# A batched matmul minus a tensor: the first eight tiles' transfers one by one in turn, transposes of tiles 3 and 4 moved into the head, and matmuls on zeros ahead of the first work

## The chip, the cores and the metric

The kernel runs on one core of one Trainium2 chip. The metric is the device time of one execution in microseconds (us); three runs of the kernel before gave a median of 220.35 us (220.28 to 220.97). A core has a matrix engine (TensorE, "PE" in the profile, its weight loads listed apart as "PEld"), a vector engine (VectorE, "DVE"), a scalar engine (ScalarE, "ACT"), GpSimd ("POOL") and a queue processor (SyncE, "SP") that here issues every transfer. 16 DMA engines move data between the chip's main memory and on-chip memory. Each engine works through its own list in order and waits on semaphores for the others.

## The reference

```python
batch, m, k, n = 16, 512, 1024, 768
# x: (16, 512, 1024), weight: (1024, 768), sub_value: (16, 512, 768), all float32
def reference(x, weight, sub_value):
    return (np.matmul(x, weight) - sub_value).astype(np.float32)
```

The 16 x 512 rows are one list of 8192 rows. The kernel casts x and the weight to 16-bit floats, multiplies with 32-bit sums and subtracts in 32 bits.

## The kernel before

**Tiles.** The 8192 rows are 64 "m tiles" of 128 rows, numbered mi from 0 to 63. Four of them are a group g, the unit of most transfers: a group of x is 2048 KB, of sub and of the output 1536 KB each, a single tile of x 512 KB and of sub 384 KB. The weight comes in four pieces (c from 0 to 3) of 768 KB; `load_w` (line 72) loads one and lets VectorE cast its two halves (line 76). The contraction of 1024 is done in four chunks c, each against one weight piece.

**One m tile** passes through five steps. `cast` (line 94): ScalarE turns the tile of x into 16-bit floats. `transposes` (line 100): TensorE transposes it in four pieces, each a multiplication with an identity matrix (line 105), into a PSUM buffer (`psum_t`, two of them); behind the fourth, ScalarE copies the result to on-chip memory (`xt_tile`, line 112). `matmuls(mi, c)` (line 128): four matmuls of 384 columns for one chunk, 16 for a tile, summed into one of three `psum_o` buffers (line 133). `finish` (line 141): VectorE subtracts, reading `psum_o` and the tile of sub and writing the result over the tile of sub (`so_tile`, line 144). `store` (line 90) sends a group of these out.

**The order** on each engine is the order in which the program names the steps; nothing is rearranged between `keep` calls. First SyncE's list of transfers is named (lines 149 to 162): x tile 0, then the weight pieces with x tiles 1 and 2 between them, x tile 3, sub 0 and 1, x 4 and 5, and so on in pairs and then in groups. Then the head (lines 164 to 183): tiles 0 to 2 (HEAD is 3) are cast, transposed and multiplied chunk by chunk as weight pieces come; when all 48 matmuls of the three are named, their subtractions follow, then cast and transposes of tiles 3 and 4, then the casts of 5 and 6. Then the tile loop (line 186), from tile 3 on: the four chunks of tile mi with one transpose piece of tile mi + 2 behind each, the copy of that tile, the cast of tile mi + 4, and the subtraction of tile mi.

**Transfers in the loop.** At the start of group g the loop names the load of x group g + 3, of sub group g + 2 and the store of group g - 1 (XA, SA, OA are 3, 2, 1). A load waits until its buffer is free (four for groups of x, six shared by sub groups and weight pieces), a store for the subtraction of the group's last tile. Besides, each transfer waits for the landing of the one eight places before it in SyncE's list, since eight semaphores are used in turn.

**The end.** The last group is stored as two tiles, one tile and one tile.

Of the kernel before, what the change touches and what calls it, by code (L numbers as in the profile page):

```python
# [8 lines left out]
P = 128  # L9
Q = 32  # L10
F32 = mybir.dt.float32
F16 = mybir.dt.float16

S = 8
G = 4
XA, SA, OA = 3, 2, 1
TA = 2
CA = 2
HEAD = 3
ON_DVE = frozenset()  # L20


@with_exitstack
def kernel(
    ctx: ExitStack,
    tc: tile.TileContext,
    x: bass.AP,
    weight: bass.AP,
    sub_value: bass.AP,
    out: bass.AP,  # L30
):
    nc = tc.nc
# [12 lines left out]
    n_c = KW // P  # L45

    x_s = x_flat.rearrange("(s p j) k -> s p j k", p=P, j=S)
    sub_s = sub_flat.rearrange("(s p j) n -> s p j n", p=P, j=S)
    out_s = out_flat.rearrange("(s p j) n -> s p j n", p=P, j=S)
    w_c = weight.rearrange("(c p r) n -> c p r n", p=P, r=2)  # L50

    def rows(view, mi, n):
        return view[mi // S][:, mi % S : mi % S + n]

    const_pool = ctx.enter_context(tc.tile_pool(name="const", bufs=1))
    w_pool = ctx.enter_context(tc.tile_pool(name="w_pool", bufs=1))
    x_pool = ctx.enter_context(tc.tile_pool(name="x_pool", bufs=4))
    x16_pool = ctx.enter_context(tc.tile_pool(name="x16_pool", bufs=CA + 2))
    xt_pool = ctx.enter_context(tc.tile_pool(name="xt_pool", bufs=TA + 3))
    so_pool = ctx.enter_context(tc.tile_pool(name="so_pool", bufs=6))  # L60
    psum_t_pool = ctx.enter_context(tc.tile_pool(name="psum_t", bufs=2, space=bass.MemoryType.PSUM))
    psum_o_pool = ctx.enter_context(tc.tile_pool(name="psum_o", bufs=3, space=bass.MemoryType.PSUM))

    ident = const_pool.tile([P, P], F32)
    make_identity(nc, ident)


    w_sb = w_pool.tile([P, n_c, 2, N], F16)

    x_t, so_t, x16_t, xt_t, ps_t, po_t = {}, {}, {}, {}, {}, {}  # L70

    def load_w(c):
        st = so_pool.tile([P, 2, N], F32, name="w_stage", tag="so_tile")
        keep(nc.sync.dma_start(out=st, in_=w_c[c]))
        for r in range(2):
            keep(nc.vector.tensor_copy(out=w_sb[:, c, r], in_=st[:, r]))  # L76

    def load_x(mi, n):
        g, j = divmod(mi, G)
        if j == 0:  # L80
            x_t[g] = x_pool.tile([P, G, K], F32, name="x_tile")
        keep(nc.sync.dma_start(out=x_t[g][:, j : j + n], in_=rows(x_s, mi, n)))

    def load_sub(mi, n):
        g, j = divmod(mi, G)
        if j == 0:
            so_t[g] = so_pool.tile([P, G, N], F32, name="so_tile")
        keep(nc.sync.dma_start(out=so_t[g][:, j : j + n], in_=rows(sub_s, mi, n)))

    def store(mi, n):  # L90
        g, j = divmod(mi, G)
        keep(nc.sync.dma_start(out=rows(out_s, mi, n), in_=so_t[g][:, j : j + n]))

    def cast(mi):
        g, j = divmod(mi, G)
        x16_t[mi] = x16_pool.tile([P, K], F16, name="x16_tile")
        keep(nc.scalar.copy(out=x16_t[mi], in_=x_t[g][:, j]))  # L97


    def transposes(mi):  # L100
        def one(c):
            def f():
                if c == 0:
                    ps_t[mi] = psum_t_pool.tile([P, K], F16, name="psum_t")
                keep(nc.tensor.transpose(  # L105
                    ps_t[mi].bitcast(F32)[:, c * P : (c + 1) * P],
                    x16_t[mi].bitcast(F32)[:, c * P : (c + 1) * P],
                    ident,
                ))
                if c == n_c - 1:  # L110
                    xt_t[mi] = xt_pool.tile([P, K], F16, name="xt_tile")
                    keep(nc.scalar.copy(out=xt_t[mi], in_=ps_t.pop(mi)))  # L112
                    x16_t.pop(mi)
            return f
        return [one(c) for c in range(n_c)]

    def transposes_dve(mi):
        xt_t[mi] = xt_pool.tile([P, K], F16, name="xt_tile")
        src = x16_t.pop(mi).bitcast(F32).rearrange("p (c q) -> p c q", c=n_c)
        dst = xt_t[mi].bitcast(F32).rearrange("p (c m) -> p c m", c=n_c)  # L120
        for a in range(P // Q):
            for b in range(P // Q):
                keep(nc.vector.transpose(
                    dst[b * Q : (b + 1) * Q, :, a * Q : (a + 1) * Q],
                    src[a * Q : (a + 1) * Q, :, b * Q : (b + 1) * Q],
                ))

    def matmuls(mi, c):
        if c == 0:
            po_t[mi] = psum_o_pool.tile([P, 2, 512], F32, name="psum_o")  # L130
        for r in range(2):
            for h in range(2):
                keep(nc.tensor.matmul(  # L133
                    po_t[mi][:, h, :NS],
                    xt_t[mi][:, 2 * P * c + r : 2 * P * (c + 1) : 2],
                    w_sb[:, c, r, h * NS : (h + 1) * NS],
                    start=(c == 0 and r == 0),
                    stop=(c == n_c - 1 and r == 1),
                ))

    def finish(mi):
        g, j = divmod(mi, G)
        o = so_t[g][:, j].rearrange("p (h n) -> p h n", h=2)
        keep(nc.vector.tensor_tensor(  # L144
            out=o, in0=po_t.pop(mi)[:, :, :NS], in1=o, op=mybir.AluOpType.subtract
        ))


    load_x(0, 1)
    for c in range(n_c):  # L150
        load_w(c)
        if c < 2:
            load_x(c + 1, 1)
    load_x(3, 1)
    load_sub(0, 2)
    load_x(4, 2)
    load_sub(2, 2)
    load_x(6, 2)
    for g in range(2, XA):
        load_x(g * G, G)  # L160
        if g - 1 < SA:
            load_sub((g - 1) * G, G)

    for mi in range(HEAD):
        cast(mi)
        for f in transposes(mi):
            f()
        for c in range(max(mi, 1)):
            matmuls(mi, c)
        if mi:  # L170
            for t in range(mi + 1):
                matmuls(t, mi)
    for c in range(HEAD, n_c):
        for mi in range(HEAD):
            matmuls(mi, c)
    for mi in range(HEAD):
        finish(mi)
    for mi in range(HEAD, HEAD + TA):
        cast(mi)
        for f in transposes(mi):  # L180
            f()
    for mi in range(HEAD + TA, HEAD + TA + CA):
        cast(mi)


    for mi in range(HEAD, n_mt):
        g, j = divmod(mi, G)
        if j == 0 or mi == HEAD:
            if g + XA < n_g:
                load_x((g + XA) * G, G)  # L190
            if g + SA < n_g:
                load_sub((g + SA) * G, G)
            if g >= OA:
                store((g - OA) * G, G)
        t = mi + TA
        tr = []
        if t < n_mt and t not in ON_DVE:
            tr = transposes(t)
        for c in range(n_c):
            matmuls(mi, c)  # L200
            if tr:
                tr[c]()
        if mi + TA + CA < n_mt:
            cast(mi + TA + CA)
        finish(mi)
        if t + 1 < n_mt and t + 1 in ON_DVE:
            transposes_dve(t + 1)
    for g in range(n_g - OA, n_g - 1):
        store(g * G, G)
    store(n_mt - G, G - 2)  # L210
    store(n_mt - 2, 1)
    store(n_mt - 1, 1)
# [30 lines left out]
```

## Time and profile before

| | |
|---|---|
| median of three runs | 220.35 us (220.28 to 220.97) |
| profiled execution: its time, its span | 221.13 us, 219.4 us |
| mean granted TensorE clock | 0.982 |
| busy: PE, ACT, DVE | 202.2 us (92%), 126.7 us (58%), 65.2 us (30%) |
| read from main memory, written | 61.87 MB, 25.17 MB |
| a chunk matmul (line 133), mean | 332 ns, x1024 |
| a transpose piece (line 105), mean | 282 ns, x256 |
| a cast (line 97), a copy (line 112), a subtraction (line 144), mean | 1048 ns, 1012 ns, 958 ns, x64 each |

The span is the time from the first to the last instruction that the profiler recorded; the execution's own time is a little longer. Matmuls are pipelined, so the time shown for one is longer than the distance from one to the next, and a group's length (first start to last end) divided by its count is the better price. The page cuts the span into 40 slices of 5.5 us with a digit for each engine's busy tenths; the granted clock of TensorE has its own row there.

### The profile page before, as it was taken

To read this page: it belongs to the slowest core of one execution; us is meant where nothing else is said; L and a number is where in the kernel's file an instruction comes from. 1 tells how busy PE (TensorE), PEld (TensorE's weight loads), DVE (VectorE), ACT (ScalarE), POOL (GpSimd) and SP (SyncE) were. 2 spreads that over 40 slices of the span, in tenths; PEclk is the share of its full clock that TensorE was granted. 3 is DMA by queue.
4 is the path that set the end of the run, shared out by engine and by line. 5 is a ranking of instruction groups with operands and counts; after the bars stand their busy time and mean duration, and the time that the engine had idled before them with its cause. 6 is when DMAs were issued, how large, how long until landed. Compare 5 with 4: busy or idle time off the path is not lost.

```text
span 219.4 us, 3000 instructions
## 1 busy us (share of the span) xinstructions
PE 202.2 (92%) x1280; PEld 138.3 (63%) x1280; DVE 65.2 (30%) x72; ACT 126.7 (58%) x129; POOL 0.7 (0%) x6
## 2 busy tenths in 40 slices
PE   0687589999999999999999999999999999999991
PEld 0344356677667766677667766677667766676660
DVE  0330403322333323333233332233322333223331
ACT  3523526666766667666667666676666766667510
POOL 1000000000000000000000000000000000000000
PEclk9999958999999999999999999999999999999999
DMA  6999999999999999999999999999999999995543
GB/s 226 422 416 420 438 427 416 432 426 418 423 419 429 423 430 427 426 425 435 427 428 430 426 417 428 435 426 424 425 434 407 429 433 426 424 424 211 251 179 143
DMA packets 8509, 87.22 MB, mean 398 GB/s; under 512 B 944, under 2 KB 944, under 8 KB 2608
## 3 DMA queue, kind: packets, MB, share of 16 engines
q1 hardware_dynamic: 8496, 87.04, 94.4%
q8 instruction: 10, 0.16, 0.3%
q14 instruction: 3, 0.02, 0.0%
HBM read 61.87 MB, written 25.17 MB: 397 GB/s over the span
## 4 chain that ended last, share of the span: by engine, by line
PE 92%; ACT 3%; DMA 2%; issue 1%; DVE 0%
PE psum_o L133 78%; PE psum_t L105 14%; DMA x_tile<-in_x_dram 2%; ACT x_tile L97 1%; ACT xt_tile L112 1%; DVE so_tile L144 0%
## 5 line engine op out<-in xcount | busy, mean ns | idle before, releaser
L133 PE MATMUL psum_o<-w_sb,xt_tile 128*128 128x384 f16 x1024 | 198.2, 332 | 3.3 <-ACT xt_tile L112 3.3
L133 PEld LDWEIGHTS <-xt_tile 128*128 128x128 f16 x1024 | 101.5, 99 | 50.0 <-ACT xt_tile L112 4.5
L112 ACT COPY xt_tile<-psum_t 128x1024 f16<-128x1024 f16 x64 | 64.8, 1012 | 80.7 <-PE psum_t L105 80.7
L144 DVE TENSOR_TENSOR so_tile<-psum_o,so_tile 128x768 f32<-128x768 f32 x64 | 61.1, 958 | 138.9 <-PE psum_o L133 138.9
L105 PE MATMUL psum_t<-ident,x_tile 128*128 128x128 f32 x256 | 69.4, 282 | 9.4 <-ACT x_tile L97 9.4
L97 ACT CAST x_tile<-x_tile 128x1024 f16<-128x1024 f32 x64 | 67.0, 1048 | 2.8 <-DMA x_tile<-in_x_dram 2.8
L105 PEld LDWEIGHTS psum_t<-ident,x_tile 128*128 128x128 f32 x256 | 37.0, 146 | 26.2 <-issue 6.8
L76 DVE CAST w_sb<-w_stage 128x768 f16<-128x768 f32 x8 | 4.1, 557 | 11.8 <-DMA w_stage<-in_weight_dram 11.8
L97 ACT ACT_TABLE_LOAD x1 | 1.3, 1283 | 0.7 <-PEq L227 0.7
masks.py:199 POOL TENSOR_SCALAR_AFFINE_SELECT ident<-ident 128x128 f32<-128x128 f32 x1 | 0.3, 294 | 0.1
masks.py:197 POOL MEMSET ident<- 128x128 f32 x1 | 0.2, 206 | 0.3 <-POOLq L227 0.3
L227 POOL MEMSET const-bfloat16-1.0<- 128x1 bf16 x1 | 0.1, 102 | 0.0
L227 POOL MEMSET const-uint8-127<- 128x1 uint8 x1 | 0.1, 102 | 0.0
L227 POOL MEMSET const-float32-0.0<- 128x1 f32 x1 | 0.1, 99 | 0.2 <-issue 0.2
L227 POOL MEMSET const-float32-1.0<- 128x1 f32 x1 | 0.1, 99 | 0.0
## 6 DMA issues: line engine op xcount, KB each, us to landing
x_tile<-in_x_dram SPq DMA_DIRECT2D x14, 2048.0 KB, 25.7
so_tile<-in_sub_value_dram SPq DMA_DIRECT2D x15, 1536.0 KB, 28.9
out_dram<-so_tile SPq DMA_DIRECT2D x15, 1536.0 KB, 21.9
w_stage<-in_weight_dram SPq DMA_DIRECT2D x4, 768.0 KB, 8.6
x_tile<-in_x_dram SPq DMA_DIRECT2D x4, 512.0 KB, 7.3
x_tile<-in_x_dram SPq DMA_DIRECT2D x2, 1024.0 KB, 14.4
so_tile<-in_sub_value_dram SPq DMA_DIRECT2D x2, 768.0 KB, 13.7
out_dram<-so_tile SPq DMA_DIRECT2D x1, 768.0 KB, 3.3
```

The lines of the kernel that those rows point to most:

```text
L76: keep(nc.vector.tensor_copy(out=w_sb[:, c, r], in_=st[:, r]))
L97: keep(nc.scalar.copy(out=x16_t[mi], in_=x_t[g][:, j]))
L105: keep(nc.tensor.transpose(ps_t[mi].bitcast(F32)[:, c * P : (c + 1) * P], x16_t[mi].bitcast(F32)[:, c * P : (c + 1) * P], ident,))
L112: keep(nc.scalar.copy(out=xt_t[mi], in_=ps_t.pop(mi)))
L133: keep(nc.tensor.matmul(po_t[mi][:, h, :NS], xt_t[mi][:, 2 * P * c + r : 2 * P * (c + 1) : 2], w_sb[:, c, r, h * NS : (h + 1) * NS], start ...
L144: keep(nc.vector.tensor_tensor(out=o, in0=po_t.pop(mi)[:, :, :NS], in1=o, op=mybir.AluOpType.subtract))
L227: nc = _bacc.Bacc("TRN2", target_bir_lowering=False, num_devices=1)
```

## The change

SyncE's list of the first transfers is now a table, `HEAD_TRANSFERS`, with a kind, a first tile and a number of tiles. Up to x tile 3 it is the order of before. Then single tiles of sub and of x alternate up to x tile 7, then pairs up to x tiles 10 and 11 and sub tiles 6 and 7. In the head, 25 matmuls of a zero tile of 512 columns against a zero tile are put before the transposes of tile 0 (13), behind them (5), and behind those of tile 1 (4) and tile 2 (3); they write to a `psum_o` buffer that nothing reads. The transposes of tile 3 now come before the last chunk of tiles 0 to 2, with each of whose chunks the tile's subtraction follows, and those of tile 4 behind that chunk. In the tile loop the store named at group g is that of group g - 2 (OA is 2), and there are seven `so_tile` buffers for six. The functions for transposing on VectorE are rewritten, but `ON_DVE` is empty in both kernels: they are not run.

```diff
-XA, SA, OA = 3, 2, 1
+XA, SA, OA = 3, 2, 2
+HEAD_TRANSFERS = [('x', 0, 1), ('w', 0, 0), ('x', 1, 1), ('w', 1, 0), ('x', 2, 1), ('w', 2, 0), ('w', 3, 0), ('x', 3, 1), ('s', 0, 1), ('x', 4, 1), ('s', 1, 1), ('x', 5, 1), ('s', 2, 1), ('x', 6, 1), ('s', 3, 1), ('x', 7, 1), ('x', 8, 2), ('s', 4, 2), ('x', 10, 2), ('s', 6, 2)]
...
-    so_pool = ctx.enter_context(tc.tile_pool(name="so_pool", bufs=6))
+    so_pool = ctx.enter_context(tc.tile_pool(name="so_pool", bufs=7))
...
-    for mi in range(HEAD):
-        cast(mi)
+    for kind, at, n in HEAD_TRANSFERS:
+        {"w": lambda: load_w(at), "x": lambda: load_x(at, n), "s": lambda: load_sub(at, n)}[kind]()
+    idle_w = const_pool.tile([P, P], F16)
+    idle_x = const_pool.tile([P, 512], F16)
+    nc.vector.memset(idle_w, 0.0)
+    nc.vector.memset(idle_x, 0.0)
+    idle_o = psum_o_pool.tile([P, 2, 512], F32, name="psum_o")
+    def idle(n):
+        for _ in range(n):
+            keep(nc.tensor.matmul(idle_o[:, 0], idle_w, idle_x, start=True, stop=True))
+    def transpose_tile(mi):
         for f in transposes(mi):
             f()
-        for c in range(max(mi, 1)):
-            matmuls(mi, c)
-        if mi:
-            for t in range(mi + 1):
-                matmuls(t, mi)
-    for c in range(HEAD, n_c):
-        for mi in range(HEAD):
-            matmuls(mi, c)
+    idle(13)
+    cast(0)
+    transpose_tile(0)
+    idle(5)
+    matmuls(0, 0)
+    cast(1)
+    transpose_tile(1)
+    idle(4)
+    matmuls(0, 1)
+    matmuls(1, 0)
+    matmuls(1, 1)
+    cast(2)
+    transpose_tile(2)
+    idle(3)
+    matmuls(0, 2)
+    matmuls(1, 2)
+    for c in range(3):
+        matmuls(2, c)
+    cast(3)
+    transpose_tile(3)
     for mi in range(HEAD):
+        matmuls(mi, 3)
         finish(mi)
-    for mi in range(HEAD, HEAD + TA):
+    for mi in range(HEAD + 1, HEAD + TA):
         cast(mi)
-        for f in transposes(mi):
-            f()
-    for mi in range(HEAD + TA, HEAD + TA + CA):
-        cast(mi)
+        transpose_tile(mi)
+    for mi in range(HEAD + TA, n_mt):
+        if mi - lead(mi) < HEAD:
+            cast(mi)
```

The rewritten head shifts line numbers: the cast is at line 108, the transposes at 116, the copy at 123, the chunk matmuls at 149, the subtraction at 160, the fillers at 177.

The end of TensorE's head before: the last two rows of the 48 matmuls (tile 2, buffer `xt_tile_159`), the transposes of tiles 3 (`x16_tile_197`) and 4 (`x16_tile_206`), and the first matmul of tile 3. "x3" counts equal rows, and the brackets name the semaphores that are waited for.

```order
L133 LDWEIGHTS xt_tile_159
L133 MATMUL psum_o_161<-w_sb_84,xt_tile_159 128x384
L105 MATMUL psum_t_199<-ident_79,x16_tile_197 128x128 [waits PE_49,Activation_49]
L105 MATMUL psum_t_199<-ident_79,x16_tile_197 128x128 x3
L105 MATMUL psum_t_208<-ident_79,x16_tile_206 128x128 [waits PE_49,Activation_49]
L105 MATMUL psum_t_208<-ident_79,x16_tile_206 128x128 x3
L133 LDWEIGHTS xt_tile_204
L133 MATMUL psum_o_223<-w_sb_84,xt_tile_204 128x384 [waits DVE_49]
```

The same engine with the change, at the transposes of tile 3 (`x16_tile_224`): ahead of them a matmul of tile 2's third chunk (`xt_tile_198`), behind them the last chunk of tile 0 (`xt_tile_153`).

```order
L149 LDWEIGHTS xt_tile_198
L149 MATMUL psum_o_211<-w_sb_90,xt_tile_198 128x384
L116 MATMUL psum_t_226<-ident_85,x16_tile_224 128x128 [waits Activation_49]
L116 MATMUL psum_t_226<-ident_85,x16_tile_224 128x128 x3
L149 LDWEIGHTS xt_tile_153
L149 MATMUL psum_o_160<-w_sb_90,xt_tile_153 128x384 [waits DVE_49]
```

Tile 3's transposes have moved from behind the last chunk's 12 matmuls to ahead of them; tile 4's (not shown) stand between those matmuls and the first one of tile 3.

SyncE's list before, from the ninth transfer on (`so_tile_106` is sub group 0, `x_tile_108` x group 1, `x_tile_112` x group 2; 1024 columns are one tile of x, 768 one of sub):

```order
L88 DMA so_tile_106<-in_sub_value_dram 128x1536 [waits DMAHW0_49]
L82 DMA x_tile_108<-in_x_dram 128x2048 [waits DMAHW1_49]
L88 DMA so_tile_106<-in_sub_value_dram 128x1536 [waits DMAHW2_49]
L82 DMA x_tile_108<-in_x_dram 128x2048 [waits DMAHW3_49]
L82 DMA x_tile_112<-in_x_dram 128x4096 [waits DMAHW4_49]
```

With the change, from the ninth on (`so_tile_112` is sub group 0, `x_tile_114` x group 1):

```order
L93 DMA so_tile_112<-in_sub_value_dram 128x768 [waits DMAHW0_49]
L87 DMA x_tile_114<-in_x_dram 128x1024 [waits DMAHW1_49]
L93 DMA so_tile_112<-in_sub_value_dram 128x768 [waits DMAHW2_49]
L87 DMA x_tile_114<-in_x_dram 128x1024 [waits DMAHW3_49]
L93 DMA so_tile_112<-in_sub_value_dram 128x768 [waits DMAHW4_49]
L87 DMA x_tile_114<-in_x_dram 128x1024 [waits DMAHW5_49]
L93 DMA so_tile_112<-in_sub_value_dram 128x768 [waits DMAHW6_49]
L87 DMA x_tile_114<-in_x_dram 128x1024 [waits DMAHW7_49]
L87 DMA x_tile_122<-in_x_dram 128x2048 [waits DMAHW0_49]
```

Four transfers of two tiles have become eight of one, with one tile of sub ahead of each tile of x; x group 2 comes in two halves.

VectorE's list with the change begins with the two memsets of the fillers' tiles; before, it began with the casts of the first weight piece (`w_stage_87`).

```order
L171 MEMSET idle_w_128 128x64
L172 MEMSET idle_x_129 128x256
L81 CAST w_sb_90<-w_stage_93 128x768 [waits DMAHW1_49]
L81 CAST w_sb_90<-w_stage_93 128x768
L81 CAST w_sb_90<-w_stage_98 128x768 [waits DMAHW3_49]
```

The casts follow behind them in their old order.

More of the change, by code (lines that the diff above doesn't have):

```diff
@@ L59 @@
     xt_pool = ctx.enter_context(tc.tile_pool(name="xt_pool", bufs=TA + 3))
[L60 removed]
+    x16p_pool = ctx.enter_context(tc.tile_pool(name="x16p_pool", bufs=2))
+    xtp_pool = ctx.enter_context(tc.tile_pool(name="xtp_pool", bufs=2))
+    so_pool = ctx.enter_context(tc.tile_pool(name="so_pool", bufs=7))
     psum_t_pool = ctx.enter_context(tc.tile_pool(name="psum_t", bufs=2, space=bass.MemoryType.PSUM))
@@ L95, in cast @@
         g, j = divmod(mi, G)
+        first = mi - mi % 2
+        if first in ON_DVE:
+            if mi == first:
+                x16_t["pair", mi] = x16p_pool.tile([P, 2, K], F16, name="x16p_tile")
+            keep(nc.scalar.copy(out=x16_t["pair", first][:, mi - first], in_=x_t[g][:, j]))
+            return
         x16_t[mi] = x16_pool.tile([P, K], F16, name="x16_tile")
@@ L195 @@
         t = mi + TA
-        tr = []
-        if t < n_mt and t not in ON_DVE:
-            tr = transposes(t)
+        tr = transposes(t) if t < n_mt and t - t % 2 not in ON_DVE else []
         for c in range(n_c):
@@ L202 @@
                 tr[c]()
-        if mi + TA + CA < n_mt:
-            cast(mi + TA + CA)
+        for t in range(mi, n_mt):
+            if t - lead(t) == mi:
+                cast(t)
         finish(mi)
-        if t + 1 < n_mt and t + 1 in ON_DVE:
-            transposes_dve(t + 1)
+        if mi + LEAD_DVE - 1 in ON_DVE:
+            waiting += transposes_dve(mi + LEAD_DVE - 1)
+        for f in waiting[:PER]:
+            f()
+        del waiting[:PER]
     for g in range(n_g - OA, n_g - 1):
```

38 lines of the change are left out of this document (16 added, 22 removed).

## The prediction

> **What bounds the kernel now.** I read the page's slices first, then the chain, then the opening of TensorE's timeline.
>
> ```profile
> span 219.4 us, 3000 instructions
> PE   0687589999999999999999999999999999999991
> PEclk9999958999999999999999999999999999999999
> DMA  6999999999999999999999999999999999995543
> q1 hardware_dynamic: 8496, 87.04, 94.4%
> PE 92%; ACT 3%; DMA 2%; issue 1%; DVE 0%
> ```
>
> From slice 7 on TensorE is full, and the chain that ends last is 92% TensorE. The 16 DMA engines are full too, until slice 36. So two resources are nearly level, and the only place with air is the first 36 us. There the timeline of TensorE (start, length, engine, line, operation, count, wait) says what happens:
>
> ```profile
> 5.97 1.09 PE L105 MATMUL psum_t<-ident,x_tile 128*128 128x128 f32 x4 [5.97 <-ACT x_tile L97]
> 8.16 1.46 PE L133 MATMUL psum_o<-w_sb,xt_tile 128*128 128x384 f16 x4 [1.10 <-ACT xt_tile L112]
> 11.58 4.02 PE L133 MATMUL psum_o<-w_sb,xt_tile 128*128 128x384 f16 x12 [1.10 <-ACT xt_tile L112]
> 15.40 1.06 PE L105 MATMUL psum_t<-ident,x_tile 128*128 128x128 f32 x4
> 17.56 5.38 PE L133 MATMUL psum_o<-w_sb,xt_tile 128*128 128x384 f16 x32 [1.10 <-ACT xt_tile L112]
> 22.77 0.60 PE L105 MATMUL psum_t<-ident,x_tile 128*128 128x128 f32 x4
> 25.42 0.66 PE L105 MATMUL psum_t<-ident,x_tile 128*128 128x128 f32 x4 [2.05 <-ACT x_tile L97]
> 25.91 0.81 PE L133 MATMUL psum_o<-w_sb,xt_tile 128*128 128x384 f16 x4
> 28.12 0.48 PE L105 MATMUL psum_t<-ident,x_tile 128*128 128x128 f32 x1 [1.40 <-ACT x_tile L97]
> 28.39 1.49 PE L133 MATMUL psum_o<-w_sb,xt_tile 128*128 128x384 f16 x4
> 36.49 0.81 PE L133 MATMUL psum_o<-w_sb,xt_tile 128*128 128x384 f16 x4
> ```
>
> Twelve matmuls take 4.02 us at 11.58, about 0.32 each, but 32 take 5.38 at 17.56, about 0.16 each: the array runs at half speed until about 17 us, whatever the clock row says there. After the waits of 2.05 and 1.40 us it drops again: four matmuls take 0.81 at 25.91 and 1.49 at 28.39. The windows (us, TensorE busy, granted clock, DMA) show that second drop:
>
> ```profile
> 22.94:28.12 5.18, 1.74 (x12) 0.91 1.03 440
> 28.12:34.10 5.98, 5.98 (x20) 0.50 1.02 427
> 36.49:48.63 12.14, 12.14 (x82) 1.00 1.01 427
> ```
>
> From 28.12 to 34.10 the clock is 0.50, which costs half of 5.98, 2.99 us; the 0.91 ahead of it puts the drop near 27.2 (5.18 x 0.09 / 0.5 is 0.93 us at half), some 6.9 us of half clock in all. From 36.49, where tile 5 begins, four tiles take 12.14 us, 3.035 a tile. The tile loop goes at this pace to the end, so what the change is worth is how much sooner tile 5 begins.
>
> **The change, part by part.** *The transfers.* Up to tile 3 of x the order of transfers is unchanged; then single tiles of sub and x alternate. SyncE's queue shows landings, because the ninth and later transfers each wait for the one eight places before:
>
> ```profile
> 0.74 0.38 SPq L82 DMA_DIRECT2D x_tile<-in_x_dram  x1
> 7.92 0.33 SPq L88 DMA_DIRECT2D so_tile<-in_sub_value_dram  x1
> 14.85 0.33 SPq L82 DMA_DIRECT2D x_tile<-in_x_dram  x1
> 16.19 0.33 SPq L88 DMA_DIRECT2D so_tile<-in_sub_value_dram  x1
> 20.54 0.33 SPq L88 DMA_DIRECT2D so_tile<-in_sub_value_dram  x1
> ```
>
> At 7.92 x tile 1 has landed, at 14.85 the last weight, at 16.19 x tile 3, at 20.54 sub tiles 0 and 1 and x tiles 4 and 5: 1.835 MB in 4.35 us, 422 GB/s. At that rate a sub tile of 0.393 MB takes 0.93 us and an x tile of 0.524 MB 1.24, so x tile 4 now lands near 18.4 (before: with tile 5, by 20.54), tile 5 near 20.5, tile 6 near 22.7, tile 7 near 24.9. No row has sub tiles one by one; the bounds for smaller pieces are no loss, and 8% (tile 3 alone, 14.85 to 16.19, took 1.34 for 1.24), 0.35 us by tile 5 and 0.7 by tile 7. I take none: it is hidden anyway, as tiles 5 and 7 have about 1 us of room before their casts below (21.5 and 25.9).
>
> *The fillers.* 13 matmuls of 512 columns stand ahead of tile 0, 12 more behind the transposes of tiles 0, 1 and 2. By columns (512/384 of the rows above) one costs 0.43 at half speed and 0.22 at full. They need two memsets on VectorE, which in the new program stand ahead of its weight casts; the nearest row is POOL's:
>
> ```profile
> 0.73 0.21 POOL masks.py:197 MEMSET ident<- 128x128 f32 x1 [0.29 <-POOLq L227]
> 6.65 1.03 DVE L76 CAST w_sb<-w_stage 128x768 f16<-128x768 f32 x2 [6.65 <-DMA w_stage<-in_weight_dram]
> 9.82 1.03 DVE L76 CAST w_sb<-w_stage 128x768 f16<-128x768 f32 x2 [2.14 <-DMA w_stage<-in_weight_dram]
> 12.98 1.03 DVE L76 CAST w_sb<-w_stage 128x768 f16<-128x768 f32 x2 [2.13 <-DMA w_stage<-in_weight_dram]
> ```
>
> Two memsets from 0.74 put the first filler near 1.2 us. If all 13 run at half speed they end at 6.8, 0.8 us after tile 0 could be transposed (5.97); if the clock rises on the way, before 5.97, at no cost. How soon it rises: from 11.58 on TensorE was busy but for one wait, and the clock was full by 17.56, 6 us of work at most; from 1.2 that is by 7.2. The other 12 lie in waits for ScalarE's copies (1.10 us each above) and for the weight casts, and cost nothing while the clock is full. Taking it as full by then: the transposes of tile 0 end near 6.6 and its copy near 7.6; the cast of tile 1, bound by its landing at 7.92, ends at 9.05. Its transposes and copy end near 10.8; the weight cast of 9.82 ends at 10.85. Twelve matmuls of 0.165 (5.38/32 and a little less) and the transposes of tile 2 end near 13.2, its copy near 14.2; the weight cast of 12.98 ends at 14.0. From 13.8, twenty matmuls end near 17.1, or 17.9 with the late bound of 0.8 us; tile 3 cannot be transposed before 17.3 (next part), so the bounds are no loss and 0.6 us, and I take no loss.
>
> *Tiles 3 and 4 inside the head.* Here ScalarE and the landing of tile 3 set the time. Before:
>
> ```profile
> 17.40 1.05 ACT L97 CAST x_tile<-x_tile 128x1024 f16<-128x1024 f32 x1
> 23.41 1.01 ACT L112 COPY xt_tile<-psum_t 128x1024 f16<-128x1024 f16 x1 [4.96 <-PE psum_t L105]
> 24.32 1.05 ACT L97 CAST x_tile<-x_tile 128x1024 f16<-128x1024 f32 x1
> 26.11 1.01 ACT L112 COPY xt_tile<-psum_t 128x1024 f16<-128x1024 f16 x1 [0.75 <-PE psum_t L105]
> 27.02 1.99 ACT L97 CAST x_tile<-x_tile 128x1024 f16<-128x1024 f32 x2
> ```
>
> Tile 3 was cast at 17.40, but its transposes stood behind all 48 matmuls of the head, so ScalarE, which is served in order, idled 4.96 us with the cast of tile 4 behind the copy. Now the same ScalarE order runs from the landing: cast of tile 3 from 16.2 to 17.25 (landing 16.19, 1.05); transposes 17.3 to 17.9 (0.60); copy from 17.95; cast of tile 4 from 18.85 (0.91 behind the copy's start, as 23.41 to 24.32) to 19.9, with its data there since 18.4. Meanwhile TensorE does 12 matmuls, 17.9 to 19.9. Transposes of tile 4 from 19.95 to 20.55; copy from 20.6; cast of tile 5 from 21.5 to 22.55; the first transpose of tile 5 at 22.6. In the profile it is at 28.12: 5.52 us gained. A wait stays: TensorE's first matmul group of tile 3 runs 20.55 to 21.2, and it then waits 1.4 us for that cast.
>
> From that transpose to tile 5 it is 28.12 to 36.49, 8.37 us, in the profile. At full clock it is two tiles less one group of four matmuls, 6.07 less 0.65 (4 x 0.162), 5.42: tile 5 at 28.02. Another 2.95 us, the half-clock loss again (2.99). **Sum: 8.47 us.**
>
> *The rest of the run.* Stores are now issued behind the loads of their turn and one buffer is added; the group that a store waits for is finished at the same tile as before, so I cost it at nothing as long as the DMA engines have a backlog. What hides it:
>
> ```profile
> 0.00:40.00 40.00, 27.27 (x131) 16.41 (x132) 9.10 (x14) 17.25 (x18) 0.70 (x6) 0.91 0.97 397
> 40.00:200.00 160.00, 160.00 (x1056) 112.17 (x1054) 50.39 (x53) 103.48 (x106) 0.00 (x0) 1.00 1.01 425
> 200.00:219.40 19.40, 14.95 (x97) 9.75 (x94) 5.75 (x6) 5.94 (x6) 0.00 (x0) 0.97 0.42 172
> 214.98 0.96 DVE L144 TENSOR_TENSOR so_tile<-psum_o,so_tile 128x768 f32<-128x768 f32 x1 [1.64 <-PE psum_o L133]
> out_dram<-so_tile SPq DMA_DIRECT2D x2, 384.0 KB, 2.3
> ```
>
> A tile needs 1.31 MB in 3.035 us, 432 GB/s, and gets 425: the loads lose 0.05 us a tile on TensorE. Counting bytes in the new order (15.9 MB by 40 us, then 0.425 MB a us), x tiles 12 to 15 land near 37 and are cast near 41; x 60 to 63 land near 178 and are wanted near 187; sub 56 to 59 land near 181.5, wanted at 186. All in time, though the margins of the profile shrink by the gain. At 200 us 3.3 MB are left, 7.8 us at full rate, so the DMA floor is 207.8 and the rest of a landing, 1.4 (2.3 less 0.9 for its bytes): 209.2. The last subtract moves from 214.98 to 206.5 and the end, 3.46 us behind its finish (215.94 to 219.4), to 210.9. The floor is close, but not reached.
>
> The profiled execution took 221.13 us, 1.73 over its span, and 0.78 over the median of 220.35. 221.13 less 8.47 is 212.7; against the median it is 211.9. I say 212.0.
>
> **The rivals.** *The clock drops again (B).* What dropped it before is in 22.94:28.12: 3.4 us idle of 5.18, in two waits. The wait of 1.10 us at 17.56, alone, did not drop it. I leave one of 1.4 us alone, at 21.2, nearer to the second. If it drops the clock, the price is between half and the whole of what the drop cost now, 6.9/2 or 3.45 us, by how long TensorE must be busy until it rises: 213.7 to 215.5, 214.6 in the middle.
> [...]
>
> *Loads too late (C).* TensorE at 432 against 425 GB/s has eaten its lead: for it, the full DMA row; against it, the margins above. If the head's transfers are a tenth slower, x 12 to 15 come 3 us later and the room is gone; TensorE then waits 1 to 2 us: 213 to 214.
>
> *Zeros do not wake the clock (D), slower.* If the array's activity is judged by data, 13 fillers end at 6.8 and the 12 others cost 5.1 us at 0.43 on the path. Added up at 0.32 a matmul and 1.06 per four transposes, the twenty matmuls of tile 2's group begin near 20.4; as in the profile the clock is full after 5 to 6 us of work, near 25.6, when 16 of them are done; the rest, tiles 3 and 4 and the cast of tile 5 as above put its first transpose near 31.6 and tile 5 at 37.0, 0.5 later than now: 220.9. With the wait for that cast dropping the clock once more, 3 us on top, 224. It decides from the point where the matmuls near 11 us still take 0.32. Nothing in the profile speaks for it; no row has zeros.
>
> *The fillers are in the way (E).* The clock is full, but they overrun their waits: at most 0.8 us, which is within the forecast's own range, 211.0 to 213.0.
>
> **How the numbers follow.** Forecast with E 0.62, B 0.20, C 0.10, D with the second drop 0.05, D without it 0.03. The range takes in B and C: up to 215.5, B's upper end, and down to 210.6, half-way from the forecast's own lower end to the DMA floor (209.2 of span, 210.2 against the median). The likeliest case's own range is 211.0 to 213.0: the sum, 1 us early or late. Some 0.3%, 0.7 us, is what a measurement here can tell from no change: faster 0.92 (forecast, B, C), same 0.03 (D without the drop), slower 0.05.
>
> **What would show it.** Matmuls of the groups near 11 us at 0.16 each; the first transpose of tile 5 near 22.6 with a wait of about 1.4; tile 5's matmuls at 28; 3.035 a tile thereafter with no wait of ScalarE for x; last subtract near 206.5. B shows as a clock of 0.5 after 22 us, C as ScalarE waiting for x after 27 us, D as 0.32 a matmul at 11 us. The forecast is wrong if tile 5 begins after 30 us, or if TensorE waits in the tile loop.

## The result and the profile after

The changed kernel takes 212.84 us (median of 4, 212.71 to 213.49) against 220.31 (220.22 to 220.97): a ratio of 0.966, with a 95% interval of 0.9633 to 0.9687. Its profiled execution took 212.81 us with a span of 211.0, where 210.9 had been forecast.

TensorE's timeline of the changed kernel, from the fillers (line 177) to tile 5 (start, length, engine, line, operation, count, wait):

```profile
1.26 5.19 PE L177 MATMUL psum_o<-idle_x,idle_w 128*128 128x512 f16 x13 [1.26 <-DVE idle_x L172]
6.29 0.60 PE L116 MATMUL psum_t<-ident,x_tile 128*128 128x128 f32 x4
10.43 2.25 PE L149 MATMUL psum_o<-w_sb,xt_tile 128*128 128x384 f16 x12
13.60 3.54 PE L149 MATMUL psum_o<-w_sb,xt_tile 128*128 128x384 f16 x20
17.25 0.65 PE L116 MATMUL psum_t<-ident,x_tile 128*128 128x128 f32 x4
17.74 2.11 PE L149 MATMUL psum_o<-w_sb,xt_tile 128*128 128x384 f16 x12
19.95 0.66 PE L116 MATMUL psum_t<-ident,x_tile 128*128 128x128 f32 x4
20.44 0.81 PE L149 MATMUL psum_o<-w_sb,xt_tile 128*128 128x384 f16 x4
22.65 0.33 PE L116 MATMUL psum_t<-ident,x_tile 128*128 128x128 f32 x1 [1.40 <-ACT x_tile L108]
28.13 0.81 PE L149 MATMUL psum_o<-w_sb,xt_tile 128*128 128x384 f16 x4
```

The matmuls near 11 us are at full speed (12 in 2.25 us), tile 3 is transposed at 17.25, tile 5 for the first time at 22.65 behind a wait of 1.40 us, and tile 5's matmuls begin at 28.13, 8.36 us sooner than the 36.49 of before. The windows (from and to; length; busy time and count of PE, PEld, DVE, ACT, POOL; granted clock; DMA share; GB/s) show the clock at 1.00 after these waits, and the end:

```profile
25.00:30.00 5.00, 5.00 (x35) 3.50 (x34) 0.96 (x1) 3.63 (x4) 0.00 (x0) 1.00 1.01 420
200.00:206.00 6.00, 6.00 (x40) 3.77 (x38) 1.92 (x2) 1.01 (x1) 0.00 (x0) 1.00 0.92 388
206.00:211.00 5.00, 0.59 (x4) 0.13 (x2) 0.96 (x1) 0.00 (x0) 0.00 (x0) 0.96 0.45 179
```

The kernel before had 0.72 in the first of these stretches. At its end the transfers had caught up with TensorE and waited for its tiles, in the same stretch (200 to 206 us) and as far ahead of the end as that stretch now lies (208.4 to 214.4 us):

```profile
25.00:30.00 5.00, 3.18 (x15) 1.94 (x16) 0.00 (x0) 3.27 (x4) 0.00 (x0) 0.72 1.00 425
200.00:206.00 6.00, 6.00 (x42) 4.21 (x40) 1.92 (x2) 3.92 (x4) 0.00 (x0) 1.00 0.23 93
208.40:214.40 6.00, 6.00 (x39) 3.79 (x38) 1.92 (x2) 1.01 (x1) 0.00 (x0) 1.00 0.43 177
```

The chain of the changed kernel that ended last (start, length, what; its first long pieces, in order of time) begins with a transfer, not with TensorE:

```profile
4.22 11.90 DMA x_tile<-in_x_dram
16.15 1.05 ACT x_tile L108
17.25 0.67 PE psum_t L116 x4
18.84 1.06 ACT x_tile L108
19.95 0.67 PE psum_t L116 x4
20.67 0.88 issue
21.55 1.06 ACT x_tile L108
```

This is the landing of x tile 3, its cast, its transposes, the cast and transposes of tile 4, the cast of tile 5. Fillers and the chunks of the head are not on it.

### The profile page after: what moved, and what is told of

Read it like the earlier page. It is cut to its first block, busy times and chain, and to the rows that moved or that the text cites. A ratio compares the mean times of both kernels' runs of the same rounds, so it can differ in the third digit from the quotient of the medians.

```text
span 211.0 us, 3061 instructions
## 1 busy us (share of the span) xinstructions
PE 203.5 (96%) x1305; PEld 138.2 (66%) x1305; DVE 65.5 (31%) x74; ACT 127.1 (60%) x129; POOL 0.7 (0%) x6
## 4 chain that ended last, share of the span: by engine, by line
PE 88%; DMA 6%; ACT 2%; SPq 2%; issue 1%; DVE 0%
PE psum_o L149 75%; PE psum_t L116 13%; DMA x_tile<-in_x_dram 6%; ACT x_tile L108 2%; SPq L79 1%; SPq L87 1%; DVE so_tile L160 0%; ACT xt_tile L123 0%
## 5 line engine op out<-in xcount | busy, mean ns | idle before, releaser
L149 PE MATMUL psum_o<-w_sb,xt_tile 128*128 128x384 f16 x1024 | 193.3, 326 | 0.0
L149 PEld LDWEIGHTS <-xt_tile 128*128 128x128 f16 x1024 | 100.1, 98 | 44.2 <-issue 0.6
L116 PE MATMUL psum_t<-ident,x_tile 128*128 128x128 f32 x256 | 67.6, 273 | 1.8 <-ACT x_tile L108 1.6
L116 PEld LDWEIGHTS psum_t<-ident,x_tile 128*128 128x128 f32 x256 | 35.4, 141 | 18.8 <-ACT x_tile L108 3.3
L177 PE MATMUL psum_o<-idle_x,idle_w 128*128 128x512 f16 x25 | 8.3, 486 | 1.3 <-DVE idle_x L172 1.3
L81 DVE CAST w_sb<-w_stage 128x768 f16<-128x768 f32 x8 | 4.1, 556 | 10.6 <-DMA w_stage<-in_weight_dram 10.6
L177 PEld LDWEIGHTS <-idle_w 128*128 128x128 f16 x25 | 3.0, 119 | 4.9 <-issue 3.2
```

Of the source, the lines that this page charges most:

```text
L116: keep(nc.tensor.transpose(ps_t[mi].bitcast(F32)[:, c * P : (c + 1) * P], x16_t[mi].bitcast(F32)[:, c * P : (c + 1) * P], ident,))
L149: keep(nc.tensor.matmul(po_t[mi][:, h, :NS], xt_t[mi][:, 2 * P * c + r : 2 * P * (c + 1) : 2], w_sb[:, c, r, h * NS : (h + 1) * NS], start ...
L177: keep(nc.tensor.matmul(idle_o[:, 0], idle_w, idle_x, start=True, stop=True))
```

## The experiments

The change has three parts for the head: fillers, order (older tiles' chunks first, tile 3's transposes ahead of the last chunk) and transfers. The theory was that all three are needed; the rivals gave the gain to one of them.

**No fillers.** The change without its 25 matmuls on zeros:

```diff
-    idle(13)
     cast(0)
     transpose_tile(0)
-    idle(5)
     matmuls(0, 0)
... (and without idle(4), idle(3), their two tiles and memsets)
```

> The change without its 25 matmuls on zeros; transfers, transposes and stores as changed. My theory: TensorE is at half clock until some 17 us, as before, so twelve matmuls near 11 us take 4.0 us instead of 2.25, the transposes of tile 3 come near 20.5 to 21 instead of 17.25, and tile 5 begins 3.5 us later than with the change: 216.3 us; if the wait ahead of tile 5 then drops the clock too, 218 to 219.8. Rival 1, the whole gain is the clock: 220.3. Rival 2, the gain is all order and transfers: 212.8.

213.23 us (212.73 to 213.58; ratio to before 0.9666, 0.9627 to 0.9705): the fillers bring nothing that can be told here, and the theory's 216.3 was wrong. TensorE's timeline without them:

```profile
6.08 1.09 PE L116 MATMUL psum_t<-ident,x_tile 128*128 128x128 f32 x4 [6.08 <-ACT x_tile L108]
8.27 1.46 PE L149 MATMUL psum_o<-w_sb,xt_tile 128*128 128x384 f16 x4 [1.10 <-ACT xt_tile L123]
9.53 1.06 PE L116 MATMUL psum_t<-ident,x_tile 128*128 128x128 f32 x4
10.57 2.92 PE L149 MATMUL psum_o<-w_sb,xt_tile 128*128 128x384 f16 x12
13.76 3.52 PE L149 MATMUL psum_o<-w_sb,xt_tile 128*128 128x384 f16 x20
17.39 0.66 PE L116 MATMUL psum_t<-ident,x_tile 128*128 128x128 f32 x4
```

The clock is at half until 10.6, and then rises within the twelve matmuls (2.92 us, between 4.02 and 2.1 to 2.25). In the new order the chunk of tile 0 stands ahead of tile 1's, so TensorE has work while ScalarE copies, and from 8.27 on hardly waits: the clock rises some 5 us sooner than before (there four transposes at 15.40 still took 1.06), without fillers. No run has the new order of the chunks alone. The twenty matmuls end at 17.28, just before tile 3, which landed at 16.29, is ready to be transposed at 17.39. So the half-speed start is hidden behind that landing.

**Fillers alone**, in the kernel before:

```diff
+    idle(13)
     for mi in range(HEAD):
         cast(mi)
         for f in transposes(mi):
             f()
+        idle((5, 4, 3)[mi])
```

> The kernel before with only the 25 matmuls on zeros added at the same four places. My theory: the 48 matmuls of the head end near 20 instead of 23, but tile 4 is then cast behind tile 3's copy, near 21 to 22, and TensorE has two waits of about 1.9 and 1.4 us close together, as before. The first transpose of tile 5 comes near 24.7; with the clock dropping as before tile 5 begins near 33 and the time is 216.5 to 217; without a drop 214.5. Rival 1, the whole gain is the clock that the fillers raise at the start: 212.8.

216.97 us (216.57 to 217.96; ratio 0.9845, 0.9805 to 0.9885), as expected. In the old order the same fillers are worth almost 4 us: the 32 matmuls begin at 14.33 instead of 17.56, since there TensorE's own work is the path. But tile 3 stands behind them, and two waits come again, of 2.05 and 0.77 us:

```profile
19.54 0.60 PE L105 MATMUL psum_t<-ident,x_tile 128*128 128x128 f32 x4
22.19 1.09 PE L105 MATMUL psum_t<-ident,x_tile 128*128 128x128 f32 x4 [2.05 <-ACT x_tile L97]
25.33 0.47 PE L105 MATMUL psum_t<-ident,x_tile 128*128 128x128 f32 x1 [0.77 <-ACT x_tile L97]
25.59 1.49 PE L133 MATMUL psum_o<-w_sb,xt_tile 128*128 128x384 f16 x4
```

The clock had already dropped at 22.19 (1.09 for four transposes), right behind the first of the two waits, and four matmuls take 1.49.

**Transfers alone**, in the kernel before: its list of first transfers replaced by `HEAD_TRANSFERS`.

```diff
-    load_x(0, 1)
-    for c in range(n_c):
-        load_w(c)
...
+    for kind, at, n in HEAD_TRANSFERS:
+        {"w": lambda: load_w(at), "x": lambda: load_x(at, n), "s": lambda: load_sub(at, n)}[kind]()
```

> The kernel before with only the new list of first transfers. My theory: nothing gained (220.6, the kernel before's own), since before the change tile 4 was cast behind tile 3's copy at 24.3, long after its landing at 20.5, and TensorE's cold first 17 us and the second drop of the clock stay. Rival: the transfers carry the gain by themselves: 215 or less.

220.66 us against 220.43 (ratio 1.0017, 0.9987 to 1.0046): nothing, as expected.

**The change with the old transfers.**

```diff
-HEAD_TRANSFERS = [..., ('x', 3, 1), ('s', 0, 1), ('x', 4, 1), ('s', 1, 1), ('x', 5, 1), ...]
+HEAD_TRANSFERS = [..., ('x', 3, 1), ('s', 0, 2), ('x', 4, 2), ('s', 2, 2), ('x', 6, 2), ('x', 8, 4), ('s', 4, 4)]
```

> The change with the list of first transfers of before (x 4 and 5, 6 and 7 and sub in pairs, x 8 to 11 at once). My theory: tile 4 lands near 20.5 instead of 18.4 and is on the path, because its cast could start at 18.84; the first transpose of tile 5 is 1.7 us later, 24.3. If the clock holds, 214.5 us; if the now longer wait ahead of tile 4's transposes together with the 1.4 us behind drops it, 217 to 217.5. Rival: single tiles don't matter, since the cast of tile 4 was far from the landing in the kernel before (24.32 against 20.5): 212.8.

215.19 us (214.24 to 217.23; ratio 0.977, 0.9705 to 0.9834). The four executions lie at 214.24, 214.50, 215.89 and 217.23 with mean clocks of 1.000, 0.999, 0.986 and 0.982. So single transfers are worth 1.5 us as such (tile 5 is first transposed at 24.13 here, at 22.65 in the change), and they take away a wait of 1.83 us ahead of tile 4, behind which the clock drops in some executions. Only the one that held it (214.24) has a trace; that two of the others lost it is read from their mean clocks:

```profile
17.48 2.11 PE L149 MATMUL psum_o<-w_sb,xt_tile 128*128 128x384 f16 x12
21.42 0.66 PE L116 MATMUL psum_t<-ident,x_tile 128*128 128x128 f32 x4 [1.83 <-ACT x_tile L108]
24.13 0.33 PE L116 MATMUL psum_t<-ident,x_tile 128*128 128x128 f32 x1 [1.40 <-ACT x_tile L108]
```

**Order alone**: no fillers and the old transfers (the two edits above together).

> The change without fillers and with the old list of transfers: only the order in the head is new (older tiles' chunks first, tile 3's transposes ahead of the last chunk). After the run without fillers (213.2 in place of 212.8) my theory is that the landing of tile 3 at 16.2 and not the fillers sets the time of the head in this order, so that this run is that with the old transfers (215.2, between 214.2 and 217.2 by whether the clock drops) and at most 0.5 more: 215.2 to 216. Rival: fillers or single transfers are needed for the order to bring anything: 218 or more.

216.17 us (214.42 to 217.35; ratio 0.9806, 0.9751 to 0.9861), with clocks of 1.000 down to 0.980 by execution: 0.2 us above what was expected, and below the rival's 218. So the order alone brings about 4 us, and up to 6 where the clock holds. The profiled execution (216.57) lost the clock right behind its first wait: the transposes there are slowed, and four matmuls take 1.48.

```profile
21.48 0.80 PE L116 MATMUL psum_t<-ident,x_tile 128*128 128x128 f32 x4 [1.91 <-ACT x_tile L108]
22.08 1.48 PE L149 MATMUL psum_o<-w_sb,xt_tile 128*128 128x384 f16 x4
```

**Tile 3's transposes at their old place**, everything else as changed:

```diff
-    cast(3)
-    transpose_tile(3)
     for mi in range(HEAD):
         matmuls(mi, 3)
         finish(mi)
-    for mi in range(HEAD + 1, HEAD + TA):
+    for mi in range(HEAD, HEAD + TA):
         cast(mi)
         transpose_tile(mi)
```

> The change with cast and transposes of tile 3 behind the last chunk of tiles 0 to 2, where they were before; fillers and transfers as changed. My theory: the last chunk ends near 19.2, tile 3 is transposed to 19.8, copied to 20.8, tile 4 cast to 21.7: waits of about 2 and 1.4 us as before, first transpose of tile 5 near 24.4. 214.6 us if the clock holds, 217 to 217.6 if the two waits drop it as they did before. Rival: the place of the transposes doesn't matter once the clock is full: 212.8.

216.24 us (214.22 to 216.77; ratio 0.9788, 0.9733 to 0.9844), between the two cases that were expected. TensorE's timeline of the profiled execution:

```profile
18.81 0.60 PE L116 MATMUL psum_t<-ident,x_tile 128*128 128x128 f32 x4
21.46 0.66 PE L116 MATMUL psum_t<-ident,x_tile 128*128 128x128 f32 x4 [2.05 <-ACT x_tile L108]
24.16 0.47 PE L116 MATMUL psum_t<-ident,x_tile 128*128 128x128 f32 x1 [1.40 <-ACT x_tile L108]
24.43 1.49 PE L149 MATMUL psum_o<-w_sb,xt_tile 128*128 128x384 f16 x4
```

The waits are those of before, the first transpose of tile 5 comes 1.5 us later than with the change, and the clock has dropped (1.49 for four matmuls). The execution of 214.22 had a clock of 1.000: there only the 1.5 us is lost. So with these waits the clock drops in three of four executions here (mean clocks of 0.980, 0.982 and 0.987), and in all of the kernel before (0.980 to 0.982).

**Late fillers.** To see whether the waits make the drop, they were filled with matmuls on zeros, first in the kernel before, then in the kernel of the last run:

```diff
     cast(mi)
+    if mi == HEAD + 1:
+        idle(8)
     for f in transposes(mi):
         f()
...
         for c in range(n_c):
             matmuls(mi, c)
+            if mi == HEAD and c == 0:
+                idle(5)
```

> The kernel before with matmuls on zeros in its two late waits only: eight behind the transposes of tile 3, five behind the first chunk of tile 3; nothing else changed. My theory: the two waits of 2.05 and 1.40 us drop the clock near 27 us, which costs 3 to 3.5 us; with the waits filled the clock stays 1.0 and it takes 217.3, without a change in the order of anything. Rival: the drop is not made by these waits (it comes by itself, or zeros don't hold the clock): 220.5, with 0.5 in the clock row.

> The change with tile 3's transposes at their old place, and with eight and five matmuls on zeros more in its two late waits. Without those its runs lay between 214.2 (clock 1.00) and 216.8 (0.98). My theory: all runs now lie near 214.3 with a clock of 1.0. Rival: the drop is not made by the waits: the same spread, 214.2 to 216.8.

The kernel before takes 217.83 us with them (217.56 to 218.17; ratio 0.9881, 0.9859 to 0.9903), and each of the four executions has a mean clock of 0.995 or more, where each of before has 0.980 to 0.982. The other kernel takes 214.35 (214.07 to 214.56), all at 0.998 or more: the upper part of the spread without late fillers (214.22 to 216.77) is gone. Its timeline shows what is left of the wait for tile 4, 0.32 us for 2.05, and that the transposes of tile 4 come no sooner:

```profile
18.75 0.60 PE L116 MATMUL psum_t<-ident,x_tile 128*128 128x128 f32 x4
19.18 1.89 PE L177 MATMUL psum_o<-idle_x,idle_w 128*128 128x512 f16 x8
21.39 0.66 PE L116 MATMUL psum_t<-ident,x_tile 128*128 128x128 f32 x4 [0.32 <-ACT x_tile L108]
```

So it is the waits that drop the clock, matmuls on zeros in them hold it, and in the kernel before the drop is worth 2.8 us. Both waits were filled together, so these runs don't say which of the two counts.

**Tile 3 later.** If the landing of tile 3 sets the head, a delay of it must come through:

```diff
-('x', 3, 1), ('s', 0, 1), ('x', 4, 1)
+('s', 0, 1), ('x', 3, 1), ('x', 4, 1)
```

> The change with x tile 3 behind sub tile 0 in the list of transfers, so that it lands 0.94 us later; all landings from x tile 4 on are as they were. My theory: the landing of tile 3 sets the head; tile 5 begins 0.9 us later (29.0) and the time is 213.7. Rival: TensorE's own work up to 17.3 sets it, or the DMA engines set the end whatever the head does: 212.8 to 213.1.

213.58 us (213.50 to 213.76; ratio 0.9686, 0.9671 to 0.9702). TensorE's timeline of it at tiles 3 and 5:

```profile
18.12 0.66 PE L116 MATMUL psum_t<-ident,x_tile 128*128 128x128 f32 x4 [1.09 <-ACT x_tile L108]
23.53 0.33 PE L116 MATMUL psum_t<-ident,x_tile 128*128 128x128 f32 x1 [1.40 <-ACT x_tile L108]
```

These come at 17.25 and 22.65 in the change, and the last subtract moves from 206.62 to 207.50: 0.87 to 0.88 us at each point, and 0.7 at the end of the span (211.0 to 211.7).

**The old stores**: `OA = 1` and six `so_tile` buffers in the change.

> The change with the stores and buffers of before: the store of group g - 1 named at group g, ahead of nothing but behind the loads of its own turn, and six so_tile buffers. My theory: no difference (212.8, within 0.7), because the DMA engines have a backlog all the time and the order of loads and stores only moves landings by one store, 3.7 us, while x tiles land some 9 us before they are wanted. Rival: with stores ahead of the loads, x and sub come late for the sooner TensorE, ScalarE or TensorE waits in the tile loop and it takes 214 to 217.

213.03 us (212.66 to 213.16; ratio 0.9668, 0.9631 to 0.9704): no difference. With them VectorE waits for sub far more often, TensorE does not wait for it. The waits of this run, then of the change (engine, line, waited for, total, times, longest):

```profile
DVE so_tile L160 <- DMA so_tile<-in_sub_value_dram: 47.7, 15, 5.4
```

```profile
DVE so_tile L160 <- DMA so_tile<-in_sub_value_dram: 8.2, 3, 4.3
```

**A sooner tile 5.** The cast of tile 5 goes to VectorE, to take it out of ScalarE's chain; and then the same kernel with the store of one group left out, whose rows it does not write.

```diff
     for mi in range(HEAD):
         matmuls(mi, 3)
+        if mi == 2:
+            x16_t[5] = x16_pool.tile([P, K], F16, name="x16_tile")
+            keep(nc.vector.tensor_copy(out=x16_t[5], in_=x_t[1][:, 1]))
         finish(mi)
... (and no cast(5) on ScalarE; second run:)
-            if g >= OA:
+            if g >= OA and g - OA != 7:
```

> The change with the cast of tile 5 on VectorE, ahead of the subtraction of tile 2, in place of ScalarE behind tile 4's copy. My theory: the first transpose of tile 5 comes near 21.5 instead of 22.65, then TensorE waits some 0.4 us for tile 6, which lands near 23; tile 5's matmuls begin 0.8 us sooner and the last subtract is near 205.8. The DMA engines end near 209 by their bytes, so the gain reaches the end: 212.0. Rival: the DMA engines bound the end now that the change has used up the room: 212.6 or more, with the last stores landing later behind the last subtract.

> The run with tile 5 cast on VectorE (213.16), with the store of group 7 left out: the rows of that group are not written. 1.57 MB less, 3.7 us of the DMA engines' time, and nothing else. My theory: the DMA engines now set the end, so with less to move the end follows the last subtract by 3.4 us again, as in the kernel before, instead of 4.2: span near 210.5, 212.3 us. Rival: the tail behind the last subtract is not a matter of the backlog: 213.1.

With the cast on VectorE it takes 213.16 us (213.08 to 213.68; ratio 0.9682, 0.9645 to 0.9718), no better than the change: the theory's 212.0 was wrong, the rival right. TensorE's timeline of it:

```profile
21.39 0.33 PE L116 MATMUL psum_t<-ident,x_tile 128*128 128x128 f32 x1 [0.20 <-DVE x_tile L210]
25.26 0.33 PE L116 MATMUL psum_t<-ident,x_tile 128*128 128x128 f32 x1 [0.61 <-ACT x_tile L108]
```

Tile 5 is first transposed 1.26 us sooner than in the change, but then TensorE waits for the cast of tile 6, which starts at 24.16 behind its landing (late by about 1.3 us, see the landings below); at the last subtract 0.43 us is left of the gain. And that is lost at the end. VectorE's timeline, last row:

```profile
206.19 0.96 DVE L160 TENSOR_TENSOR so_tile<-psum_o,so_tile 128x768 f32<-128x768 f32 x1 [1.64 <-PE psum_o L149]
```

Its transfers by line, the last two stores (KB each, median us to landing):

```profile
out_dram<-so_tile SPq DMA_DIRECT2D x2, 384.0 KB, 4.1
```

Its window ahead of the end:

```profile
200.00:206.00 6.00, 6.00 (x39) 3.59 (x37) 1.92 (x2) 1.01 (x1) 0.00 (x0) 1.00 0.96 405
```

The same three views of the kernel with one store less:

```profile
206.08 0.96 DVE L160 TENSOR_TENSOR so_tile<-psum_o,so_tile 128x768 f32<-128x768 f32 x1 [1.64 <-PE psum_o L149]
```

```profile
out_dram<-so_tile SPq DMA_DIRECT2D x2, 384.0 KB, 2.3
```

```profile
200.00:206.00 6.00, 6.00 (x38) 3.48 (x36) 1.92 (x2) 1.01 (x1) 0.00 (x0) 1.00 0.53 215
```

The end comes 4.2 us behind the subtract (206.19 + 0.96 to 211.4) with the full traffic, 3.2 us (206.08 + 0.96 to 210.2) with a store less; the time falls to 212.09 us (211.86 to 212.44). The subtracts stand where they were. So what the DMA engines have left to do now lies on the end. It is not that all 16 are full: with the full traffic their mean share is 0.41 from 206.0 us to the end, and only 0.29 from 207.1 to 208.0 us. The packets of the trace show a few that lag. Each transfer ends with 16 packets of 4 bytes, as many as there are engines (1040 packets under 512 B for 65 transfers); of the last store's, 13 come by 209.16 and the other three at 209.51, 209.84 and 210.10, where with a store less all 16 come between 208.88 and 209.01. In the change itself the last small stores take a median of 3.4 us to land, against 2.3 before it, but the end still follows the last subtract by 3.4 us, as before. No run of a complete kernel here is better than the change.

All kernels of the head together, medians in us; the kernel before was measured anew in each of three sets (220.92, 220.43, 220.66). Rows without the new order have the old stores, which make no difference in the change; fillers and new transfers together in the old order were not run:

| fillers | order | transfers | us |
|---|---|---|---|
| - | - | - | 220.4 to 220.9 |
| - | - | new | 220.66 |
| new | - | - | 216.97 |
| - | new | - | 216.17 |
| new | new | - | 215.19 |
| - | new | new | 213.23 |
| new | new | new | 212.84 |
| new | chunks new, tile 3 old | new | 216.24 |

## Why the prediction was right, and where it was not

The sum was right in size: 8.47 us forecast for the span, 8.4 measured (219.4 to 211.0). Step by step:

- *Tiles 3 and 4 inside the head, 5.52 us.* The chain was forecast as tile 3's transposes at 17.3, tile 4's at 19.95, tile 5's first at 22.6 with a wait of 1.4; measured 17.25, 19.95, 22.65 and 1.40. That its start is the landing of tile 3 is shown by delaying it: 0.87 to 0.88 us at each later point.
- *The clock from there on, 2.95 us.* From tile 5's first transpose to its matmuls it is 5.48 us (22.65 to 28.13), forecast 5.42. The drop it replaces is worth 2.8 us by filling the waits in the kernel before.
- *The fillers.* That they lie in waits and cost nothing held: 13 end at 6.45, tile 0 is transposed at 6.29, inside the bounds. (In the run with tile 5's cast on VectorE they end at 6.95, 0.15 past the late bound, and that was hidden too.) What the prediction had wrong is what they are for: it took TensorE's arrival at 17.1 from a clock that the fillers raise. Without them TensorE arrives at 17.28 all the same, since the new order by itself leaves it hardly a wait after 8.27; the prediction gave the order of the chunks of tiles 0 to 2 no price. So the arrival came out right for a reason that was not needed. Rival D did not happen: behind 13 matmuls on zeros and nothing else, four transposes take 0.60. Its price can't be checked; the run without any fillers is at full speed by 13.76, but has no uncounted matmuls in the way.
- *Landings.* Tiles 4 and 5 landed as forecast (18.39 and 20.65 in SyncE's queue, against 18.4 and 20.5), tile 6 did not: its cast waited until 23.84, against a landing forecast for 22.7 with 0.7 as the worst loss by tile 7, and tile 7 landed at 26.05 for 24.9. It cost nothing, because tile 6 was not transposed before 25.75. Where tile 5 was made sooner, it cost most of that gain. The trace shows what came between. From 20 to 25 us the change's transfers hold one packet of another kind (packets, MB, share of 16 engines):

```profile
q8 instruction: 1, 0.02, 1.4%
```

It has 16 KB and lasts from 21.26 to 22.36 us. In all six profiled runs with the new transfers in which it comes between 20.8 and 22.0, tile 6 lands 2.16 to 2.62 us behind the sub tile ahead of it; in the three in which it comes later (25.24, 26.85 and 32.38 us), 1.28 to 1.35. In the run with tile 5's cast on VectorE 15 of tile 6's 16 end packets come between 21.72 and 22.25 and the last at 23.61, ahead of the landing seen at 24.10: so it was probably one engine of 16 that was held up, and the load with it. In every run the packet comes when TensorE has begun 87 to 113 matmuls, so it is probably the fetch of TensorE's own next instructions, and the 25 fillers draw it forward (21.26 us with them, 26.85 without); that is argued from the counts, not tested.

- *The rest of the run at nothing.* Held: 3.035 us a tile to the end, last subtract at 206.62 (forecast 206.5), 3.4 us from its finish to the end (3.46), and the old stores make no difference.
- *The DMA floor.* "Close, but not reached" was too kind: 209.2 was worked out from bytes as if the engines could be full to the last one. The last stores can only come when their tiles are done, and with tile 5's cast on VectorE three of the 16 end packets of the very last one come 0.35 to 0.94 us behind the others: there, with the last subtract 0.43 us sooner, the span was 211.4, not less. No execution of a kernel with all its stores has a span under 210.9, so the usable floor is near 211 by these runs, where the change stands.
- *From the profile to the median.* Here lies the miss of 0.84 us: 212.0 forecast, 212.84 measured. The profiled execution of before was 0.78 above its median, and that was carried over to the changed kernel, whose profiled execution is at its median (212.81 and 212.84). By medians the gain is 7.47 us. The excess belonged to that execution: executions of the kernel before lay between 219.29 and 222.16 in the later sets.

The rivals: B did not happen in the change (1.00 in the profiled execution until TensorE's work ends; mean clock 0.994 to 1.000 in the four). The mean counts the idle end too: with tile 5's cast on VectorE it was 0.992 with 1.00 up to 206.2 us and 0.69 behind. But a drop behind the waits ahead of tiles 4 and 5 is real, as the runs with the old transfers or the old place of tile 3 show; its price was 1.7 to 3.0 us (214.24 against 215.89 and 217.23). One premise of B's chance did not hold: the wait of 1.10 us at 17.56 can't show that the clock survives it, because the transposes ahead of it still ran at half speed (1.06 for four). The kernel before with late fillers shows it: four transposes in 0.66 at 15.21, then a wait of 1.10 and full speed. C did not happen: no wait of TensorE for x in the tile loop behind the one of 1.40 us at 22.65. E's overrun was 0.3 us and hidden.

On when the clock drops and rises: in the profiled execution of the kernel before TensorE was never idle longer than 2.05 us in one piece behind the start, and the clock dropped in every execution of that kernel in the later sets (mean clock 0.980 to 0.982). With the order alone it was down 2.5 us after the last matmul at full speed (19.57 to 22.08), with only a wait of 1.91 and four transposes between. It is not the same in every execution: those of one kernel had mean clocks of 1.000 down to 0.982 (old transfers), and the same 13 fillers take 4.34 to 5.69 us by run from a start at 1.25 or 1.26. What decides it no run here shows.

## What to carry to other kernels

The gains of a change's parts don't add up. Fillers alone bring 4.0 us and the order alone 4.3, but both together 5.7; the transfers alone bring nothing, but 7.7 together with the order. The fillers help the old order, where TensorE's own work is the path, and bring nothing to the new one with single transfers, where a landing is. Price each part against the wait that ends last once the other parts are in. When a kernel at the edge of two resources is made faster at the front, look at the tail's transfers: here the change used up the room that the DMA engines had left at the end, and the next 0.43 us did not come through.

## What the runs showed of the hardware that was not expected

With two waits of 1.83 and 1.40 us and 1.3 us of work between them (old transfers), TensorE's mean clock was 1.000 and 0.999 in two executions and 0.986 and 0.982 in the other two (214.24 to 217.23 us); with waits of 2.05 and 1.40 it was 0.980 to 0.982 in all executions of the kernel before, and 0.980 to 0.987 in three of four with tile 3's transposes at the old place. In two profiled executions it was down right behind the first wait, of 2.05 (fillers alone, 1.09 for four transposes) and 1.91 us (order alone, 0.80 for four, then 1.48 for four matmuls). One of 1.40 alone did not drop it in the profiled execution of the change (1.00 from 25 to 30 us), nor did 1.09 and 1.40 with some 4 us of work between them in four executions with tile 3 later (1.000 each). Behind matmuls on zeros and nothing else the clock was up: four transposes took 0.60 us at 6.29 in the change, 1.09 at 5.97 before. In the late waits they held it (mean clocks of 0.995 or more against 0.980 to 0.982 in the kernel before). Where one 16 KB instruction packet of 1.10 us came between, x tile 6 (512 KB) landed 2.16 us behind the sub tile ahead of it (21.62 to 23.78 in SyncE's queue); tile 5 had taken 1.29 (19.36 to 20.65), and without the packet at that place tile 6 takes 1.28 to 1.35.
